# First stage of a decoder step on one core: the first two tiles become forget gates of two heads, with wider loads and one written order per engine

## Chip, cores, metric

The kernel runs on one core of a Trainium2 chip. The metric is the device time of one execution in microseconds (us); the median of the runs shown counts.

## What is computed

One inference step of a single decoder layer for 512 prompt tokens and 8 sample tokens (T = 520 columns), width 1024, all in float32. What matters here is how the layer begins:

```
cs  = silu(c)                                  # 9 conditioning vectors: one of the prompt, eight of the samples
mod = cs @ w_mod + b_mod                       # 6 parts of 1024: sh1, sc1, g1, sh2, sc2, g2
h   = rmsnorm(x) * norm1_g * (1 + sc1) + sh1
u   = h @ w_in                                 # 64 tiles of 128 columns; q, f, i, output gate of 8 heads first
```

From u come an HGRN2 recurrence of eight heads (forget gate f, query q, value i, output gate), an RG-LRU recurrence, two merge gates, the output projection, and after a second norm an MLP with a squared ReLU.

## The kernel before

Activations lie transposed, 128 features by 520 columns, in eight blocks k. Every large product is made of three products of float32r halves (high and low part), two halves of 260 columns each, so one tile of 128 output features takes 8 blocks x 6 matmuls (`products`, L112). A weight tile is loaded (`_load_w`, L72, SP's queue), its high part is a cast on ScalarE (L84) and its low part a subtraction on VectorE (L87); `take_w` (L98) keeps splits two tiles ahead of their use and loads two ahead of the splits.

The first stage is `begin` (L1537). SP's queue loads c, x (four tiles of 128 tokens) and then pieces of w_mod of 256 columns, 1 MB each, scale and shift alternately for blocks 0-1, 2-3, 4-5, 6-7 (`load_mod`, L368); between them stand the weights of the first two tiles, forget gate and query of head 0, 128 columns each. POOL's queue loads small parameters. ScalarE squares x (`norm_x`, L436), VectorE makes the inverse root by a shift and three Newton steps (`rsqrt_small`, L187), TensorE transposes x block by block (`transposed`, L449), and `normed` (L465) scales x into u, which lies in the memory of the untransposed x.

Then follow four rounds, one for each pair of blocks: `mod` (L374) multiplies shift and scale pieces with cs (16 float32 matmuls, recorded as 32), ScalarE copies the result, TensorE transposes it four times and VectorE reduces, adds the bias and multiplies by the gain (`mod_close`, L390). `affine_split` (L479) applies scale and shift: ScalarE writes the high part (L490, with a small one at L494), VectorE a full-precision copy (L495) and the low part (L496). The products of the two first tiles for one pair stand behind the conditioning of the next pair. TensorE's order in this stage is written with `behind`, an order in the program without a wait; the rest is placed by a planner from its own estimate of times. After the last products the pool of the stage is closed, the pool of the heads is opened in its memory, and `head` (L530) starts with two sigmoids on the first accumulator; the PSUM pool `pmm` holds two accumulators.

After that the order is a list of steps, one tile after the other: for each head f, q, output gate, value; after each head two tiles of the RG-LRU. Parts of a head's recurrence are put behind later tiles by `later` (L131): the key transposes (`keys`, L691, transposes at L694) three tiles after the value tile. The value tile's sample rows go through DRAM and come back broadcast to all partitions (`head_sample_v`, L557). The stores of transposed x (L539) are put behind the output-gate tile of head 0.

Of the kernel before, what the change touches and what calls it, by code (L numbers as in the profile page):

```python
# [6 lines left out]
F32 = mybir.dt.float32  # L7
F32R = mybir.dt.float32r
# [7 lines left out]
D = 1024  # L16
L = 512
# [13 lines left out]
NWM = 8  # L31
# [20 lines left out]
class Kernel:  # L52
    def __init__(self, ctx, tc, ins, outs):
# [3 lines left out]
        self.ppt_free = True  # L57
        self.rg_pending = self.turn = self.last_hi = self.split_last = None
# [19 lines left out]
    def _split_w(self, st, place, after=None, after_lo=None):  # L78
# [5 lines left out]
        ins = self.nc.scalar.copy(hi, st)  # L84
        if after:
            self.behind(ins, after)
        ins = self.nc.vector.tensor_tensor(lo, st, hi.bitcast(F32), OP.subtract)  # L87
        if after_lo:
            self.behind(ins, after_lo)
        return hi, lo  # L90

    def split_place(self):

        self.nsplit += 1
        self.places.append(self.nsplit % 4 if self.sw else 2 * (self.nsplit % 3))
        return self.places[-1]

    def take_w(self, key):  # L98
        n = self.wcur
        assert self.wspecs[n] == key, (n, self.wspecs[n], key)  # L100
        while self.wnext_split < min(n + AHEAD + 1, len(self.wspecs)):
# [7 lines left out]
        self.wcur += 1  # L109
        return self.wsplit.pop(n)  # L110
# [127 lines left out]
    def transpose_in(self, out, rows, n):  # L238

        nc = self.nc  # L240
        ps = self.pps.tile([128, 512], F32, name="ps")
        nc.tensor.transpose(ps[:, :n], rows[:n, :], self.ident[:n, :n])
        nc.vector.tensor_copy(out, ps[:, :n])

# [9 lines left out]
    def bounds(self, r):  # L254

        nc = self.nc
        pl = self.hc.tile([128, 16], F32, name="pl")
        self.transpose_in(pl, r, 16)
        hl, lam = pl[:, 0:8], pl[:, 8:16]

        sb = self.hc
        t = sb.tile([128, 10, 8], F32, name="ptmp")
        mx, e, p, lb, na, ex, s, s2, acc, d = (t[:, j] for j in range(10))
        nc.vector.tensor_copy(mx, hl)
        nc.vector.tensor_tensor(e, hl, mx, OP.subtract)
        nc.vector.tensor_scalar(d, lam, -1.0, None, OP.mult)
        nc.vector.tensor_tensor(na, lam, d, OP.min)
        nc.scalar.activation(e, e, AF.Exp)
        self.exps = nc.scalar.activation(ex, na, AF.Exp)
        nc.vector.reciprocal(p, e)  # L270
        nc.vector.tensor_tensor(p, p, e, OP.mult)
        nc.vector.tensor_tensor(lb, p, p, OP.subtract)
        self.lbf, self.lb1, self.c8, self.c8n = (sb.tile([128, 8], F32, name=n) for n in ("lbf", "lb1", "c8", "c8n"))
        nc.vector.tensor_scalar(self.lbf, lb, 1e-30, None, OP.max)
        nc.vector.tensor_scalar(self.lb1, lb, -1.0, 1.0, OP.mult, OP.add)
        self.decay = ex, s, s2, acc, d

    def decays(self):
# [23 lines left out]
    def parameters_mod_in(self, r):  # L302
        pm = self.consts.tile([128, 64], F32, name="pm")
        self.transpose_in(pm, r, 64)
        self.bmod, self.n1g, self.n2g = pm[:, 0:48], pm[:, 48:56], pm[:, 56:64]
        for part in (1, 4):
            c = self.bmod[:, part * 8:part * 8 + 8]
            self.nc.vector.tensor_scalar(c, c, 1.0, None, OP.add)

# [1356 lines left out]
```

## Time and profile before

| | us |
|---|---|
| median of 3 runs | 1012.02 (1011.67 to 1012.32) |
| profiled execution | 1012.27 |
| span of the profile | 1010.5 |
| TensorE busy in the span | 983.7 |
| VectorE, ScalarE busy | 695.6, 516.0 |

The span runs from the first to the last instruction of the profiled execution; 1.8 us of its time lie outside. PE is TensorE (PEld its weight loads), DVE VectorE, ACT ScalarE, POOL GpSimd, SP the engine whose queue issues most loads. TensorE's records are pipelined: a matmul lasts longer than the distance to the next one. The granted clock is given as a share of 2.4 GHz, 0.50 being 1.2 GHz.

### The profile page before, as it was taken

The page shows a single profiled execution, that of the slowest core. Times are in us where ns is not written, and L with a number is a line of the kernel's source. Part 1 is how long each engine was busy: PE and PEld are TensorE (multiplying, and loading weights), DVE is VectorE, ACT ScalarE, POOL GpSimd, SP SyncE. Part 2 cuts the span into 40 slices and gives each one's busy share as a digit, 9 for nine tenths or more (in the row PEclk, how much of TensorE's full clock was granted, in tenths as well). Part 3 has the DMA queues.
Part 4 walks back from the last instruction along what each step waited for, and adds up shares of the span by engine and source line. Part 5 has one row for each costly group of instructions (what it writes and reads, how often), then busy time and mean ns, then how long its engine had stood idle before and what let it go on. Part 6 is the DMA issues. An engine that isn't in the chain of part 4 may idle for free.

```text
span 1010.5 us, 23262 instructions
## 1 busy us (share of the span) xinstructions
PE 983.7 (97%) x9585; PEld 956.7 (95%) x9585; DVE 695.6 (69%) x1545; ACT 516.0 (51%) x985; POOL 108.8 (11%) x193
## 2 busy tenths in 40 slices
PE   5999999999999999999999999999999999999996
PEld 3799999999999999999999999999999999999995
DVE  6778888698878868463233348767767766768775
ACT  5444764574565456351222234466556645646653
POOL 3000000000000000120000000022321331232050
PEclk9899999999999999999999999999999999999998
DMA  9794445354343434586566756222762482283242
GB/s 299 214 261 135 123 129 143 94 154 125 113 131 115 126 91 134 189 271 208 176 188 214 232 167 182 84 84 53 174 150 79 101 197 85 65 183 68 64 84 85
DMA packets 212572, 145.78 MB, mean 144 GB/s; under 512 B 6262, under 2 KB 196878, under 8 KB 212458
## 3 DMA queue, kind: packets, MB, share of 16 engines
q1 hardware_dynamic: 202562, 132.37, 44.3%
q0 software_dynamic: 9904, 11.92, 6.2%
q8 instruction: 75, 1.23, 0.5%
q14 instruction: 31, 0.25, 0.1%
HBM read 123.61 MB, written 13.39 MB: 136 GB/s over the span
## 4 chain that ended last, share of the span: by engine, by line
PE 90%; DVE 3%; DMA 3%; SPq 2%; ACT 1%; issue 1%; DVEq 0%; ACTq 0%
PE mm L118 65%; PE ps L1151 8%; PE pt L1151 4%; PE ps L382 2%; PE pb L1151 2%; PE pb L779 1%; PE ps L628 1%; DMA wm<-in_w_mod_dram 1%; PE mm L1151 1%; PE pt L704 1%; PE pt L717 1%; SPq L75 1%; DMA wst<-in_w_in_dram 1%; DMA xT_d<-ma 1%; SPq L371 1%
## 5 line engine op out<-in xcount | busy, mean ns | idle before, releaser
L118 PE MATMUL mm<-h,whi 128*128 128x260 f32 (+1 forms) x3072 | 508.4, 285 | 1.9 <-ACT X L157 1.2
L118 PEld LDWEIGHTS mm<-h,whi 128*128 128x128 f32 x3072 | 426.3, 189 | 6.8 <-ACT whi L84 1.7
L118 PE MATMUL mm<-h,wlo 128*128 128x260 f32 (+1 forms) x1536 | 314.6, 284 | 0.0
L84 ACT CAST whi<-wst 128x1024 fp32r<-128x1024 f32 x166 | 173.7, 1049 | 211.7 <-PE mm L118 172.5
L87 DVE TENSOR_TENSOR wlo<-wst,whi 128x1024 fp32r<-128x1024 f32 x166 | 202.6, 1221 | 88.3 <-ACT whi L84 87.1
L118 PEld LDWEIGHTS mm<-h,wlo 128*128 128x128 f32 x1536 | 239.8, 189 | 0.1
L118 PE MATMUL mm<-a,whi 128*128 128x260 f32 x512 | 82.8, 283 | 0.0
L118 PEld LDWEIGHTS mm<-a,whi 128*128 128x128 f32 x512 | 70.3, 188 | 0.9 <-issue 0.8
L118 PE MATMUL mm<-a,wlo 128*128 128x260 f32 x256 | 51.7, 284 | 0.0
L1247 DVE TENSOR_TENSOR f<-f 128x260 f32<-128x260 f32 x64 | 27.3, 427 | 28.9 <-ACT f L1242 28.2
L880 POOL DMA_DIRECT2D t<-oaT_d x8 | 4.3, 551 | 375.5 <-DMA oaT_d<-e 368.8
L1236 ACT ACTIVATE ft<-ft,fsh 128x512 f32<-128x512 f32 (+2 forms) x36 | 24.0, 676 | 35.9 <-DVE ft L1233 35.9
L1239 POOL TENSOR_TENSOR ft<-ft,fsh 128x8 f32<-128x8 f32 x28 | 18.5, 660 | 216.1 <-DVE ft L1233 216.1
L118 PE MATMUL mm<-b,whi 128*128 128x260 f32 x256 | 41.6, 284 | 0.0
L118 PEld LDWEIGHTS mm<-a,wlo 128*128 128x128 f32 x256 | 39.4, 188 | 0.0
L118 PEld LDWEIGHTS mm<-b,whi 128*128 128x128 f32 x256 | 35.0, 188 | 2.5 <-issue 2.5
L614 DVE TENSOR_TENSOR Y<-Y,tb 128x512 f32<-128x512 f32 x40 | 27.5, 688 | 11.0 <-ACT Y L616 5.5
L896 DVE TENSOR_TENSOR t<-mm,t 128x520 f32<-128x520 f32 x8 | 5.6, 701 | 37.0 <-PE mm L118 37.0
L1281 POOL DMA_DIRECT2D ma<-snap x28 | 26.1, 932 | 39.8 <-issue 22.3
L1263 POOL DMA_DIRECT2D ma<-snap x28 | 26.1, 932 | 39.0 <-DMA ma<-snap 22.5
L1242 ACT ACTIVATE f<-ft 128x520 f32<-128x520 f32 (+1 forms) x36 | 20.8, 587 | 15.0 <-POOL ft L1240 13.0
L573 ACT ACTIVATE st<-st,fkq 128x128 f32<-128x128 f32 x64 | 19.6, 389 | 14.3 <-DVE fkq L553 12.9
(508 smaller groups left out, 1819.5 us busy)
## 6 DMA issues: line engine op xcount, KB each, us to landing
wst<-in_w_in_dram SPq DMA_DIRECT2D x64, 512.0 KB
wm<-in_w_mod_dram SPq DMA_DIRECT2D x8, 2048.0 KB
wst<-in_w_ff_dram SPq DMA_DIRECT2D x64, 256.0 KB
wst<-in_w_ff_dram SPq DMA_DIRECT2D x32, 512.0 KB
wm<-in_w_mod_dram SPq DMA_DIRECT2D x8, 1024.0 KB
st<-in_state_hgrn_dram SPq DMA_DIRECT2D x8, 512.0 KB
vb<-vd SPq DMA_DIRECT2D x8, 512.0 KB
out_dram<-st SPq DMA_DIRECT2D x8, 512.0 KB
```

The lines of the kernel that those rows point to most:

```text
L84: ins = self.nc.scalar.copy(hi, st)
L87: ins = self.nc.vector.tensor_tensor(lo, st, hi.bitcast(F32), OP.subtract)
L118: self.last_product = self.nc.tensor.matmul(ps[:, s, :c.stop - c.start], x, y[:, c], start=first and n == 0, stop=last and n == 2)
L382: ins = nc.tensor.matmul(ps[r:r + 32, j * n:j * n + n], self.cT[:, k, :], w[:, k, :], start=k < 4, stop=k >= KO - 4)
L573: nc.scalar.activation(st[:, b], st[:, b], AF.Copy, scale=fkq[:, 0, b:b + 1])
L614: made = nc.vector.tensor_tensor(view(Y, b, 0, 2 * b, n, b), view(X, b, 0, 2 * b, n, b), fac, OP.mult)
L1151: ins = self.nc.tensor.matmul(ps, x[:, w], y[:, f], start=j in (1, 7, 2) and k == 0 and n == 0, stop=k == 3 and n == 2, skip_group_check=True)
L1236: nc.scalar.activation(t[:, :p], t[:, :p], AF.Relu, bias=sh[:, 0:1])
L1242: nc.scalar.activation(f, self.two(self.ft)[:, a:a + n], AF.Square)
L1247: self.nc.vector.tensor_tensor(f[:, n], f[:, a], f[:, b], op)
L1263: nc.gpsimd.dma_start(x[1][:, b], v[:, :n], accum_op=OP.add)
L1281: nc.gpsimd.dma_start(x[t][:, a], s[p], accum_op=OP.add)
```

## The change

The first two tiles are the forget gates of heads 0 and 1, whose weights are one load of 256 columns; the query of head 0 becomes the third tile, the first that is taken from the list. The conditioning weights come in pieces of 512 columns: scale of blocks 0 to 3, shift of blocks 0 to 3, (the gate weights,) scale of blocks 4 to 7, and shift of 4-5 and of 6-7 in two halves. Each piece is a session of its own (`session`, `closed`). x is transposed as its tiles arrive, six blocks at once and two later; the root comes from ScalarE's table with one Newton step. The small parameters are transposed into one PSUM tile and copied together. All instructions of the stage on TensorE, ScalarE and VectorE stand in one written order per engine (`order`), in which the products are spread over the sessions. The first weight tile of the list (query of head 0) is split before the last pair of blocks (`split_ahead`). The pool `whe`, the third place of split weights, is opened after the stage, in its memory. The key transposes of head 0 are put two tiles after the value tile. The stores of x stay behind the output gate of head 0, now the second tile after the stage.

The core of the diff:

```diff
-        self.places.append(self.nsplit % 4 if self.sw else 2 * (self.nsplit % 3))
+        self.places.append(self.nsplit % 4 if self.sw else 2 * ((self.nsplit - 1) % 3))
...
-        while self.wnext_split < min(n + AHEAD + 1, len(self.wspecs)):
+        self.split_ahead(min(n + AHEAD + 1, len(self.wspecs)))
+        self.wcur += 1
+        return self.wsplit.pop(n)
+
+    def split_ahead(self, count):
+
+        while self.wnext_split < count:
...
+        order("p", nc.tensor.transpose(ps[:, :16], rl, self.ident[:16, :16]))
+        order("p", nc.tensor.transpose(ps[:, 16:80], rm, self.ident[:64, :64]))
+        order("v", nc.vector.tensor_copy(pl, ps[:, :16]))
+        order("v", nc.vector.tensor_copy(pm, ps[:, 16:80]))
...
+        for r, n in ((ra, 57), (rb, 64), (rc[:, 0], 96), (rc[:, 1], 96)):
+            order("p", nc.tensor.transpose(ps[:, c:c + n], r, self.ident[:n, :n]))
+            c += n
+        order("v", nc.vector.tensor_copy(pa, ps[:, :313]))
...
+        mm = [self.pmm.tile([128, 2, 512], F32, name="mm") for _ in range(2)]
+        rows = [mm[0][:, 0], mm[0][:, 1], mm[1][:, 0], mm[1][:, 1],
+                self.ppb.tile([128, 512], F32, name="pb"), self.ppt.tile([128, 512], F32, name="pt")]
+        for t in range(NC):
+            for k, p in enumerate(rows):
+                order("p", nc.tensor.transpose(p[:, t * 128:(t + 1) * 128], self.xn[:, t, k * 128:(k + 1) * 128], self.ident))
+            if t == 2:
+                between()
...
+        order("a", nc.scalar.activation(r, ss, AF.Sqrt, bias=self.epsc, scale=1.0 / D))
+        h = self.sm.tile([128, 16], F32, name="rs16_h", bufs=2)[:, :8]
+        order("v", nc.vector.tensor_scalar(h, ss, -0.5 / D, -0.5 * EPS, OP.mult, OP.add))
+        self.copied("v", 4, rows[4], order)
+        order("v", nc.vector.reciprocal(r, r))
+        t = self.sm.tile([128, 16], F32, name="rs16_t", bufs=2)[:, :8]
+        order("v", nc.vector.tensor_tensor(t, r, r, OP.mult))
+        order("v", nc.vector.tensor_tensor(t, t, h, OP.mult))
+        order("v", nc.vector.scalar_tensor_tensor(r, t, 1.5, r, OP.add, OP.mult))
...
+        hi = lambda j: order("a", nc.scalar.activation(self.h_hi[:, k0 + j, :L], u[:, k0 + j, :L], AF.Identity,
+                                                       bias=sh[:, j, 0:1], scale=sc[:, j, 0:1]))
+        full = lambda j: order("v", nc.vector.tensor_scalar(f[:, j, :L], u[:, k0 + j, :L], sc[:, j, 0:1], sh[:, j, 0:1], OP.mult, OP.add))
+        lo = lambda j: order("v", nc.vector.tensor_tensor(self.h_lo[:, k0 + j, :T], f[:, j], self.h_hi[:, k0 + j, :T].bitcast(F32), OP.subtract))
+        order("v", nc.vector.tensor_tensor(f[:, :, L:], u[:, ks, L:T], sc[:, :, 1:9], OP.mult))
+        order("v", nc.vector.tensor_tensor(f[:, :, L:], f[:, :, L:], sh[:, :, 1:9], OP.add))
+        hi(0)
+        full(0)
+        order("a", nc.scalar.copy(self.h_hi[:, ks, L:T], f[:, :, L:]))
+        hi(1)
+        between(0)
+        full(1)
+        lo(0)
+        lo(1)
+        between(1)
...
-    def head(self, h, first=None):
+    def head(self, h):
         nc = self.nc
         kf, kq, kv, kg = ([x] for x in self.head_cols(h))
         st = self.head_load(h)
-        f, X = self.head_f(h, first[0] if first else self.gemm(kf, self.h)[:, :, :HALF])
-        q = self.head_q(X[:, 2], first[1] if first else self.gemm(kq, self.h)[:, :, :HALF])
+        f, X = self.first_f[h] if h < 2 else self.head_f(h, self.gemm(kf, self.h)[:, :, :HALF])
+        q = self.head_q(X[:, 2], self.gemm(kq, self.h)[:, :, :HALF])
         ps = self.gemm(kg, self.h)[:, :, :HALF]
-        if first:
+        if h == 0:
...
-        self.later(3, keys)
+        self.later(3 if h else 2, keys)
...
-            steps.append(([kf, kq, kg, kv][2 if h == 0 else 0:], self.head_start if h == 0 else self.head, h))
+            steps.append(([kf, kq, kg, kv][1 if h < 2 else 0:], self.head, h))
...
+        def order(engine, ins):
+            if engine in ends:
+                self.behind(ins, ends[engine])
+            ends[engine] = ins
+            return ins
...
+        def session(part, k0):
+            w = loaded.pop((part, k0))
+            n = w.shape[2]
+            ps = self.pps.tile([128, 512], F32, name="ps")[:, :n]
+            for k in range(KO):
+                r = 32 * (k % 4)
+                order("p", nc.tensor.matmul(ps[r:r + 32], self.cT[:, k, :], w[:, k, :], start=k < 4, stop=k >= KO - 4))
+            ev = self.sm.tile([128, 512], F32, name="modev", bufs=1)[:, :n]
+            order("a", nc.scalar.copy(ev, ps))
+            return ev, part, k0, n // 128
...
+        load(1, 0, 4)
+        load(0, 0, 4)
+        raw = self.start.tile([128, KO, 256], F32, name="wf")
+        nc.sync.dma_start(raw, self.i["w_in"][0][:, D:D + 256].rearrange("(k p) n -> p k n", p=128))
+        load(1, 4, 4)
+        load(0, 4, 2)
+        load(0, 6, 2)
...
+        order("a", self.cond())
+        order("a", nc.scalar.activation(self.act0, self.act0, AF.Sqrt))
+        ss = self.norm_x(order)
...
+        scaled(0, 1, 2, 3)
+        a = session(1, 0)
+        closed(*a)
+        scaled(4, 5, 6, 7)
+        exps()
+        order("a", nc.scalar.activation(self.act0, self.act0, AF.Sigmoid))
+        bounds_end()
+        a = session(0, 0)
+        closed(*a)
+        self.parameters_in(*par, order)
+        high(0)
...
+        self.affine_split(0, order, weights)
+        products((0, 0), (0, 1))
+        a = session(1, 4)
+        self.affine_split(2, order)
+        products((1, 0), (1, 1))
+        closed(*a)
+        a = session(0, 4)
+        products((0, 2))
+        closed(*a)
+        products((0, 3), (1, 2), (1, 3))
+        self.affine_split(4, order)
+        a = session(0, 6)
+        self.last_hi, self.split_last = ends["a"], ends["v"]
+        self.split_ahead(1)
+        ends.update(self.split_ins)
+        products((0, 4), (1, 4))
+        closed(*a)
+        self.affine_split(6, order)
+        products((0, 5), (1, 5), (0, 6), (0, 7), (1, 6), (1, 7))
...
+        self.whe = self.early.enter_context(self.tc.tile_pool(name="whe", bufs=1))
         self.hg = self.open_pool("hg", 2)
-        self.ppt_free = False
+        self.first_f = [self.head_f(h, acc[h][:, :, :HALF]) for h in range(2)]
```

## Rows read from the trace of the kernel before

**Rows 1.** Busy time by stage: window, us, engines (instructions), granted clock, DMA, GB/s.
```profile
27.50:51.00 23.50, 22.69 (x208) 17.66 (x208) 16.72 (x53) 10.67 (x18) 0.04 (x1) 0.90 0.66 197
51.00:120.00 69.00, 67.67 (x827) 66.74 (x828) 52.90 (x157) 35.66 (x80) 0.71 (x3) 1.00 0.61 176
```

**Rows 2.** Timeline of TensorE: start, us, line, tiles, count, idle time before and releaser.
```profile
25.58 1.11 PE L397 MATMUL pt<-ident,modev 128*128 128x128 f32 x4 [3.81 <-ACT modev L385]
...
35.08 1.93 PE L382 MATMUL ps<-wm,cT 128*32 128x256 f32 x32
...
49.24 0.64 PE L118 MATMUL mm<-h,whi 128*128 128x260 f32 x4
...
49.96 0.65 PE L118 MATMUL mm<-h,whi 128*128 128x260 f32 x4
...
52.08 0.75 PE L118 MATMUL mm<-h,whi 128*128 128x260 f32 x4 [1.24 <-ACT X L157]
```

**Rows 3.** Chain of waits up to 130 us: start, us, what.
```profile
17.23 10.16 DMA wm<-in_w_mod_dram
...
27.53 3.64 PE ps L382 x32
...
47.94 2.92 PE mm L118 x22
```

**Rows 4.** Busy time in short windows, around the second conditioning.
```profile
24.00:26.00 2.00, 0.42 (x2) 0.42 (x3) 2.00 (x4) 1.53 (x2) 0.00 (x0) 0.84 1.09 348
26.00:28.00 2.00, 1.17 (x12) 0.60 (x14) 2.00 (x6) 0.00 (x0) 0.00 (x0) 0.50 1.09 348
...
32.00:34.00 2.00, 2.00 (x18) 2.00 (x18) 0.86 (x6) 0.11 (x1) 0.00 (x0) 0.95 1.09 346
```

**Rows 5.** The same, a load of 512 columns and then one of 128.
```profile
535.00:536.00 1.00, 1.00 (x11) 1.00 (x10) 0.00 (x0) 0.00 (x0) 0.00 (x0) 1.00 1.06 403
...
539.00:540.00 1.00, 1.00 (x10) 1.00 (x10) 0.47 (x1) 0.00 (x0) 0.00 (x0) 1.00 1.20 295
```

**Rows 6.** Timeline of ScalarE: last square of x, copy after the third conditioning.
```profile
10.67 1.06 ACT L443 ACTIVATE ht<-xn 128x1024 f32<-128x1024 f32 x1 [0.34 <-DMA xn<-in_x_prompt_dram]
...
37.14 0.59 ACT L385 COPY modev<-ps 128x512 f32<-128x512 f32 x1 [1.12 <-PE ps L382]
```

**Rows 7.** Groups by form, 19 to 51 us: busy us, mean ns, idle before.
```profile
L490 ACT ACTIVATE h<-xn,modT 128x512 fp32r<-128x512 f32 x8 | 6.5, 814 | 8.9 <-DVE modT L409 8.9
...
L496 DVE TENSOR_TENSOR h<-ht,h 128x520 fp32r<-128x520 f32 x8 | 5.5, 699 | 0.9 <-ACT h L494 0.8
...
L477 DVE TENSOR_TENSOR xn<-ma,c 128x520 f32<-128x520 f32 x8 | 5.0, 689 | 0.0
...
L495 DVE TENSOR_SCALAR ht<-xn,modT 128x512 f32<-128x512 f32 x8 | 4.0, 543 | 0.0
...
L1557 DVE TENSOR_TENSOR wlo<-wst,whi 128x1024 fp32r<-128x1024 f32 x2 | 2.4, 1218 | 0.0
...
L385 ACT COPY modev<-ps 128x512 f32<-128x512 f32 x4 | 2.3, 585 | 2.9 <-PE ps L382 2.9
L1556 ACT CAST whi<-wst 128x1024 fp32r<-128x1024 f32 x2 | 2.1, 1036 | 1.1 <-DMA wst<-in_w_in_dram 1.1
...
L402 DVE TENSOR_REDUCE modT<-pt 128x18 f32<-128x72 f32 x8 | 1.5, 227 | 3.7 <-PE pt L397 3.7
L1577 ACT ACT_TABLE_LOAD x1 | 1.3, 1283 | 0.0
...
L405 DVE TENSOR_TENSOR modT<-modT,pm 128x36 f32<-128x36 f32 x4 | 0.8, 196 | 0.1
```

**Rows 8.** Head 0: copy of the value tile, broadcast (chain of waits), key transposes.
```profile
63.91 0.59 ACT L549 COPY e<-mm 128x520 f32<-128x520 f32 x1 [2.54 <-PE mm L118]
...
71.36 5.96 DMA vb<-vd
...
85.18 0.49 PE L694 MATMUL pt<-ident,X 128*128 128x128 f32 x3
```

More of the change, by code (lines that the diff above doesn't have):

```diff
@@ L30 @@
 SESSION = 500
-NWM = 8
 WST = 2
@@ L481, in affine_split @@
+        self.copied("a", 5, rows[5], order)
+        mm = self.pmm.tile([128, 2, 512], F32, name="mm")
+        for j in range(2):
+            for t in range(NC):
+                order("p", nc.tensor.transpose(mm[:, j, t * 128:(t + 1) * 128], self.xn[:, t, (6 + j) * 128:(7 + j) * 128], self.ident))
+        for j in range(2):
+            self.copied("a", 6 + j, mm[:, j], order)
+    def affine_split(self, k0, order, between=lambda j: None):
         nc = self.nc
@@ L1569, in begin, with load @@
-        for k in (4, 6):
-            load_mod(1, k)
-            load_mod(0, k)
-        squares = self.norm_x()
-        self.transposed()
-        self.bounds(pl)
-        self.parameters_mod_in(pm)
-        self.normed()
-        ready = nc.scalar.activation(self.act0, self.act0, AF.Sigmoid)
-        self.behind(self.behind(ready, squares), self.exps)
-        first = [first_w(st) for st in staged]
-        par = self.parameters()
+        loaded = {}
+        def load(part, k, n):
+            loaded[part, k] = w = self.start.tile([128, KO, n * 128], F32, name=f"wm{part}{k}")
+            c = part * D + k * 128
+            nc.sync.dma_start(w, self.i["w_mod"][0][:, c:c + n * 128].rearrange("(k p) n -> p k n", p=128))
@@ new lines, in begin @@
+        load(1, 0, 4)
[5 more added lines that the diff above has]
+        load(0, 6, 2)
+        first = [[self.start.tile([128, KO, 128], F32R, name=f"w{n}{j}") for n in ("hi", "lo")] for j in range(2)]
+        part = lambda j: raw[:, :, j * 128:j * 128 + 128]
+        high = lambda j: order("a", nc.scalar.copy(first[j][0], part(j)))
@@ new lines, in begin, with parameters @@
+        low = lambda j: order("v", nc.vector.tensor_tensor(first[j][1], part(j), first[j][0].bitcast(F32), OP.subtract))
+        order("a", self.cond())
+        order("a", nc.scalar.activation(self.act0, self.act0, AF.Sqrt))
+        ss = self.norm_x(order)
+        bounds = []
+        def parameters():
+            bounds.append(self.parameters_first(pl, pm, order))
+        rows = self.transposed(parameters, order)
+        exps, bounds_end = self.bounds(bounds[0], order)
+        self.normed(ss, rows, order)
@@ L1597, in begin, with weights @@
-        products(sorted(todo))
-        self.parameters_in(*par)
+                self.products(acc[j], (wh[:, k], wl[:, k]), self.h[k], k == 0, k == KO - 1, after=ends["p"])
+                ends["p"] = self.last_product
+        def weights(j):
+            if j == 0:
+                low(0)
+            else:
+                high(1)
+                low(1)
+        self.affine_split(0, order, weights)
+        products((0, 0), (0, 1))
+        a = session(1, 4)
+        self.affine_split(2, order)
```

204 lines of the change are left out of this document (80 added, 124 removed).

## The prediction

> **What bounds the kernel now.** I first read the busy times by stage. From 51 to 120 us TensorE is busy 67.67 of 69.0 us, while before that the stage of the change costs 51 us for two accumulated tiles [rows 1]. So time can only be won or lost where the first two tiles are finished and handed on; what follows is TensorE work that the change leaves alike, six matmuls per block of 128 rows, 0.72 us from one block to the next (49.24 to 49.96) [rows 2]. Then the chain of waits: it runs on a load of the conditioning weights until 27.39, on the second conditioning from 27.53 (3.64 us), and from there on TensorE alone until the last first product at 50.86 [rows 3]. The next matmul starts at 52.08, released by the second sigmoid of ScalarE [rows 2]. So two things bound the stage: arrivals until 27.4, and TensorE's order after it. The clock is a third: TensorE waited 3.81 us before 25.58, the granted clock fell in that stretch and came back around 32 (0.84, 0.50, 0.95) [rows 2, 4], and the second conditioning took 3.64 instead of the 1.93 us of the third [rows 2, 3].
>
> **Loads.** The bytes up to the end of the first weights are the same: 2.2 MB of x and c, 4.2 MB of conditioning, 1.05 MB of gate weights; before, these were all there at 27.39 [rows 3]. Their rows get longer. Rows of 1 KB moved at 348 GB/s [rows 4], a block of 512 columns (2 KB rows) at 403, weights of 128 columns (512 B rows) at 295 [rows 5]. 4.2 MB at 403 instead of 348 is 10.4 instead of 12.05 us; 1.05 MB at 348 instead of 295 is 3.0 instead of 3.55. So the wide gate weights land about 2.1 earlier, at 25.3 (27.39 less 2.1), the shift half 3.0 before that, at 22.3, the scale half 5.2 earlier still, at 17.1. Then scale of blocks 4 to 7 at 30.5, the halves of its shift at 33.5 and 36.5, and the first weight of the next tile at 38.2. The Trainium skill (DMA: Bandwidth & Descriptors, Specifications) gives some 358 GB/s as one core's share of HBM; by that the 2 KB rows would win some 0.35 us in place of 1.65. The 403 of [rows 5] speaks against the page, and the measurement decides.
>
> **What is hidden ahead of 22.3.** The squares of x end at 11.8 before, the last begun at 10.67 [rows 6]; the Sqrt table goes ahead of them, one load of 1.28 [rows 7] in a ScalarE that then waits less, so I take 12.0. The root by table with four small operations replaces twelve small ones. From 12.0 to the closing of the shift at 25.4 VectorE has three copies of 0.7, some sixteen small operations of 0.2, eight scalings (5.0 [rows 7]) and 0.7 of closing: 11 us in 13.4. Two more table loads (Exp, Sigmoid) fall between the two conditionings. I cost all this at nothing: the load of the shift covers it, with 2.4 us to spare; if shift landed earlier than 20, VectorE's 11 us would set the start instead. The parameter transposes (four tiles, one copy) move ahead of the products; they are costed below. Their eight loads are earlier in program order on POOL's queue only. The stores of x on SP's queue move behind one more product tile; weights are requested two ahead of them.
>
> **From 22.3 on**, with 0.05 for each hand-over and the pieces from [rows 2, 7]. Conditioning 1.93, copy 0.59, four transposes 0.5 (1.11 at the half clock), four of the parameters 0.5: 25.9. Reduction and bias are done by then; VectorE's copy of the parameters (313 columns, not in the trace: between the 0.2 of a small operation and the 0.7 of 520 columns; 0.45) ends at 26.4. ScalarE's cast of the gate weights ends then too (25.3 + 1.04). VectorE, in its written order: two small 0.35, full 0.5, low weights 1.22, full 0.5, two lows 0.7 each: 30.4. The products (0,0), (0,1) end at 30.9.
>
> Conditioning of scale 4 to 7: 30.9 to 32.9 (landed 30.5). Its copy stands ahead of the next high parts on ScalarE, 33.5; high 0.81, small 0.2, high 0.81: 35.3; low 36.05. Closing of scale: reduction of four blocks (two cost 0.23; I take 0.3), bias 0.2, gain 0.2: 36.75; closing of shift 0.45: 37.2. High, small, high of blocks 4 and 5 to 39.3, the lows to 40.0. TensorE meanwhile, from 32.9: two products, four transposes, a half conditioning 0.97, one product, two transposes, three products, 38.9, then the last half conditioning, 39.9.
>
> Its copy (256 columns, 0.36) 40.3. **Here the change adds a wait**: the cast of the next tile's weight (1.04, to 41.3) stands ahead of the last high parts on ScalarE, and its low part (1.22, to 42.6) ahead of the last closing on VectorE. Closing 0.45: 43.0. Highs 0.81, 0.2, 0.81; VectorE 0.35, 0.5, 0.5, lows 0.7 and 0.7: 45.1 and 45.8. TensorE has run out of products at 43.0 and waits for these two: (0,6) ends 45.6, (0,7) 46.3, (1,6) and (1,7) 47.8. A matmul outlasts its spacing by 0.16 (0.65 for four that start 0.12 apart), and the copy after the third conditioning began 0.13 after its end at 37.01 [rows 2, 6], not 0.05, which comes three times: **48.2**.
>
> **Sum.** 48.2 instead of 50.86: -2.66. The pause after it (1.22: the pool of the first stage is closed first, so both sigmoids wait for the last product) stays; the weight split early was needed then anyway. 1012.27 of the profiled execution becomes 1009.6; it lies 0.25 above the median of the runs, so **1009.4**. What a measurement of this kernel tells from no change is about 0.2%, 2.0 us. Loads an us earlier or later move the end by about as much (the wait at 30.9 has 0.4 of slack), so this case alone spans 1008.2 to 1010.4. Chance 0.52.
>
> **Rivals.**
> Half clock. TensorE has next to nothing from 25.9 to 29.7 (two matmuls near 27.4). Before, after 3.81 us without work, the clock was at 0.50 until about 32 [rows 2, 4]. If it falls here too, the conditioning of scale takes 3.64 for 1.93, and the products beside it twice their time; +1.7 and +0.6 of it reach the end: 50.5, 1011.7. The same if the clock is still low at 22.3. The Trainium skill (TensorE: Matmul & The Clock Gate, HAM oscillation) says that bursts of matmuls parted by waits for loads begin each time at the half clock, and by it this case is the forecast; the trace agrees for the one gap that was empty, while this gap is not empty. Against it, too: the changed kernel has no empty wait over 2.2 us. Chance 0.24.
>
> Long rows bring nothing. If 403 holds only beside a running TensorE stream, everything that waits for loads comes 1.6 later: 49.8, 1011.0. For it: early in the kernel small loads share the engines. Against it: the rows are the same blocks of the same matrix. The 358 GB/s of the Trainium skill's DMA page would lead nearly here. Chance 0.12.
>
> **Slower.** The value tile of head 0 becomes the third tile after the hand-over instead of the second, while its keys stay at the same tile (two later instead of three). Before, its copy at 63.91 and the key transposes at 85.18 are 21.3 apart, with a broadcast of 5.96 in between [rows 8]. One tile less, 8 x 0.72 = 5.8, leaves 15.5. If the whole chain needs its 21.3, TensorE stands 5.8 at the transposes: 1009.4 + 5.8 = 1015.2. From 4.7 of stall on it is slower than before by over 0.2%. Against it: the transposes are put where their data is expected, other tiles can go first, and the broadcast waited behind other requests. Chance 0.07.
>
> No written order in effect, or the release not tied to the whole pool: then the pause of 1.22 goes too and 1008.0 comes out, or nothing at all changes. Chance 0.05.
>
> **Numbers.** Faster by over 0.2% (below 1010.0): four fifths of the forecast's case, a quarter of the load case and half of the last, 0.47. Slower (over 1014.0): 0.07 for the stall. Within 0.2%: the half clock and the rest, 0.46. The range leaves out the stall and the tail of the half-clock case (both conditionings cold): 1007.6 to 1012.9; the likeliest case alone 1008.2 to 1010.4.
>
> **What would show it.** The first conditioning matmuls near 17, the second near 22.3, both released by a load; some 400 GB/s from 10 to 20 us; the first products at 27.4 and 29.7; a wait of TensorE for low parts near 43 to 45; the last first product near 48.2 and the next tile 1.2 later. The forecast is wrong if the granted clock is 0.50 anywhere between 29 and 34, if shift lands after 24, or if TensorE stands over 1 us between 50 and 100.

## The result and the profile after

The changed kernel takes 1014.15 us (median of 11 runs, 1012.55 to 1016.0) beside 1011.85 (1011.35 to 1012.89) for the kernel before on the same chip: a ratio of 1.0022, interval 1.0015 to 1.003. It is slower by 2.3 us; 1009.4 was forecast, with a range of 1007.6 to 1012.9: the time moved the other way and lies outside the range. The profiled execution is the slowest of the eleven (1016.0, span 1014.1).

The busy times on the page of the changed kernel, beside 983.7, 695.6 and 516.0 before:

```profile
PE 985.5 (97%) x9537; PEld 954.6 (94%) x9537; DVE 693.4 (68%) x1529; ACT 519.1 (51%) x991; POOL 108.8 (11%) x193
```

The timeline of TensorE, changed kernel: the root's transposes, the first and second conditioning, the first products, the third conditioning, two waits for the last pair of blocks, and the first matmul of the next tile, as in [rows 2].

```profile
13.31 1.09 PE L480 MATMUL pb<-ident,rs_y 128*128 128x128 f32 x4 [2.14 <-DVE rs_y L473]
...
16.50 3.35 PE L1583 MATMUL ps<-wm,cT 128*32 128x512 f32 x16
...
22.61 3.47 PE L1583 MATMUL ps<-wm,cT 128*32 128x512 f32 x16 [1.39 <-DMA wm<-in_w_mod_dram]
...
28.95 0.59 PE L121 MATMUL mm<-h,whi 128*128 128x260 f32 x2 [0.90 <-ACT h L500]
31.58 0.80 PE L121 MATMUL mm<-h,whi 128*128 128x260 f32 x2 [2.04 <-DVE h L503]
...
34.05 3.12 PE L1583 MATMUL ps<-wm,cT 128*32 128x512 f32 x16
...
48.48 0.50 PE L121 MATMUL mm<-h,whi 128*128 128x260 f32 x2 [0.67 <-ACT h L500]
49.45 0.51 PE L121 MATMUL mm<-h,whi 128*128 128x260 f32 x2 [0.46 <-DVE h L503]
...
53.59 0.75 PE L121 MATMUL mm<-h,whi 128*128 128x260 f32 x4 [1.24 <-ACT X L160]
```

Its windows of 1 us (columns as in [rows 1]; the clock is the third number from the end):

```profile
12.00:13.00 1.00, 0.00 (x0) 0.00 (x0) 0.93 (x6) 0.95 (x2) 0.00 (x0) 0.80 1.08 381
16.00:17.00 1.00, 1.00 (x7) 0.29 (x9) 1.00 (x2) 0.47 (x1) 0.00 (x0) 0.50 1.04 387
21.00:22.00 1.00, 0.23 (x3) 0.00 (x0) 0.67 (x4) 0.99 (x3) 0.00 (x0) 1.00 1.08 355
24.00:25.00 1.00, 1.00 (x10) 0.27 (x4) 0.92 (x4) 0.00 (x0) 0.00 (x0) 0.50 1.05 380
28.00:29.00 1.00, 0.10 (x2) 0.05 (x1) 0.92 (x5) 0.91 (x2) 0.00 (x0) 1.00 1.04 384
30.00:31.00 1.00, 0.00 (x0) 0.00 (x0) 1.00 (x3) 0.76 (x1) 0.00 (x0) 0.50 1.09 349
34.00:35.00 1.00, 1.00 (x9) 0.30 (x12) 0.48 (x2) 0.00 (x0) 0.00 (x0) 0.50 1.08 345
37.00:38.00 1.00, 1.00 (x11) 0.91 (x8) 0.00 (x0) 0.71 (x2) 0.00 (x0) 1.00 1.21 290
```

Its chain of waits up to the hand-over, as in [rows 3]:

```profile
4.11 18.37 DMA wm<-in_w_mod_dram
22.61 3.49 PE ps L1583 x16
...
34.12 3.04 PE ps L1583 x16
...
45.01 0.96 ACT whi L82
46.00 1.23 DVE wlo L85
49.45 2.92 PE mm L121 x22
```

Read together: the loads came as forecast. The shift weights landed at 22.48 (4.11 + 18.37), and the long rows moved at 375 to 391 GB/s in eight of the ten windows from 10 to 20, instead of 348 [rows 4]. But the granted clock, once up again after each fall, fell three times: in the window from 12, before 24 and before 30. The first fall lies within a wait of TensorE of 2.14 us, the second just behind one of 1.39 us, and the third at a single pair of matmuls that stands between waits of 0.90 and 2.04 us. The clock of 0.50 from 30 to 36 is one of the signs that the prediction named for being wrong. The conditionings that should take 1.93 took 3.35, 3.47 and 3.12. The last first product ended at 52.37 (49.45 + 2.92), not at 48.2, and 1.24 later the next tile began: the **hand-over**, 53.59 instead of 52.08.

In the table, "behind" is the span less the hand-over, that is, everything that the change was not about. Hand-over and "behind" are those of one profiled execution each; the times are medians of 5 to 11 runs (one run for the second profile of the kernel before). The rows come from several chips, so compare the ratios, which are to the kernel before on the same chip, rather than the times.

| run | hand-over | behind | time | ratio (interval) |
|---|---|---|---|---|
| before | 52.08 | 958.4 | 1011.85 | |
| before, second profile | 50.96 | 958.4 | 1011.2 (one) | |
| changed | 53.59 | 960.5 | 1014.15 | 1.0022 (1.0015 to 1.003) |
| changed, again | 53.17 | 959.1 | 1014.16 | 1.0026 (1.0017 to 1.0035) |
| all gaps filled | 49.72 | 958.8 | 1010.59 | 0.9989 (0.998 to 0.9997) |
| last gap filled | 50.92 | 958.8 | 1011.88 | 0.9999 (0.999 to 1.0008) |
| early gaps filled | 51.84 | 959.0 | 1013.21 | 1.0017 (1.0008 to 1.0026) |
| before, gap filled | 50.93 | 958.7 | 1011.55 | 1.0001 (0.9991 to 1.001) |
| forget gate and query | 53.88 | 959.1 | 1013.75 | 1.0016 (1.0007 to 1.0025) |
| state scaling later | 53.90 | 957.8 | 1013.79 | 1.0015 (1.0007 to 1.0024) |
| filled, split late | 49.10 | 957.9 | 1008.85 | 0.9974 (0.9964 to 0.9983) |
| filled, new order | 48.03 | 960.8 | 1010.18 | 0.9987 (0.9978 to 0.9996) |
| new order alone | 51.23 | 963.0 | 1014.86 | 1.0034 (1.0022 to 1.0047) |
| filled, new order, state later | 48.10 | 958.0 | 1007.9 | 0.9964 (0.9952 to 0.9977) |

### The profile page after: what moved, and what is told of

Same layout as the page of the kernel before. It is cut to its first block, busy times and chain, and to the rows that moved or that the text cites. A ratio compares the mean times of both kernels' runs of the same rounds, so it can differ in the third digit from the quotient of the medians.

```text
span 1014.1 us, 23153 instructions
## 1 busy us (share of the span) xinstructions
PE 985.5 (97%) x9537; PEld 954.6 (94%) x9537; DVE 693.4 (68%) x1529; ACT 519.1 (51%) x991; POOL 108.8 (11%) x193
## 4 chain that ended last, share of the span: by engine, by line
PE 88%; DVE 4%; ACT 3%; DMA 2%; issue 1%; SPq 0%; DVEq 0%; ACTq 0%; POOLq 0%
PE mm L121 64%; PE ps L1165 8%; PE pt L1165 4%; PE pb L1165 2%; DMA wm<-in_w_mod_dram 2%; PE ps L384 1%; PE pb L793 1%; PE ps L642 1%; PE ps L1583 1%; PE mm L1165 1%; DVE wlo L85 1%; PE pt L718 1%; PE pt L731 1%; PE pt L733 1%; DMA st<-in_state_hgrn_dram 1%
## 5 line engine op out<-in xcount | busy, mean ns | idle before, releaser
L121 PEld LDWEIGHTS mm<-a,wlo 128*128 128x128 f32 x256 | 39.4, 188 | 0.0
L1295 POOL DMA_DIRECT2D ma<-snap x28 | 26.6, 948 | 40.2 <-issue 22.3
L1277 POOL DMA_DIRECT2D ma<-snap x28 | 26.1, 932 | 39.4 <-DMA ma<-snap 22.8
```

The source lines that it names most:

```text
L121: self.last_product = self.nc.tensor.matmul(ps[:, s, :c.stop - c.start], x, y[:, c], start=first and n == 0, stop=last and n == 2)
L1277: nc.gpsimd.dma_start(x[1][:, b], v[:, :n], accum_op=OP.add)
L1295: nc.gpsimd.dma_start(x[t][:, a], s[p], accum_op=OP.add)
```

## Experiments on the clock

A filler is a matmul that nothing reads: the identity times the conditioning vectors, 256 columns, into a PSUM tile that is free then. It stands in TensorE's written order where TensorE waited.

**All gaps filled.** Four fillers before the root's transposes, two before and five behind the first conditioning, one behind the second, five before the first products.

```diff
+        def filler(dm, n):
+            for _ in range(n):
+                order("p", nc.tensor.matmul(dm[:, :256], self.ident, self.cT.rearrange("p k b -> p (k b)"), start=True, stop=True))
+        filler(self.pps.tile([128, 512], F32, name="ps"), 4)
...
+        dm = self.ppb.tile([128, 512], F32, name="pb")
+        filler(dm, 2)
         a = session(1, 0)
         closed(*a)
+        filler(dm, 5)
...
         a = session(0, 0)
+        filler(dm, 1)
         closed(*a)
         self.parameters_in(*par, order)
+        filler(dm, 5)
```

> The changed kernel with matmuls of no use (identity by the conditioning vectors, into a free PSUM tile) put where TensorE waits: 4 after the first transposes of x, 2 before the first conditioning, 5 before the second, 1 after it, 5 before the first products. Theory 'clock' (the three stretches at the half clock set the end of the stage): the granted clock stays at 1.00 from about 20 us on, the second and third conditionings take 1.9 instead of 3.5 and 3.1 us, the last first product ends at 48.2 to 49.2 instead of 52.4, and the time falls by about 3 us, to 1011. Rival 'order' (the written order and its waits set the end, whatever the clock): the clock is at 1.00, but the last first product stays beyond 51 and the time at 1013 to 1014.

Windows and timeline of TensorE with all gaps filled (the windows as above, then the second and third conditioning, the last products and the next tile):

```profile
24.00:25.00 1.00, 0.99 (x6) 0.30 (x2) 0.00 (x0) 0.53 (x1) 0.00 (x0) 1.00 1.05 385
28.00:29.00 1.00, 0.77 (x5) 0.51 (x3) 1.00 (x2) 1.00 (x2) 0.00 (x0) 1.00 1.04 384
30.00:31.00 1.00, 1.00 (x9) 1.00 (x10) 1.00 (x2) 0.00 (x0) 0.00 (x0) 1.00 1.09 347
```

```profile
22.43 1.92 PE L1583 MATMUL ps<-wm,cT 128*32 128x512 f32 x16 [0.98 <-DMA wm<-in_w_mod_dram]
...
31.37 1.92 PE L1583 MATMUL ps<-wm,cT 128*32 128x512 f32 x16
...
48.08 0.40 PE L121 MATMUL mm<-h,wlo 128*128 128x260 f32 x2
49.72 0.75 PE L121 MATMUL mm<-h,whi 128*128 128x260 f32 x4 [1.24 <-ACT X L160]
```

The clock stays at 1.00, every conditioning takes 1.92, and the last first product ends at 48.48 (48.08 + 0.40; 48.2 was forecast for a full clock). 1010.59 is 3.6 us less than the changed kernel, on another chip; by the ratios it is 3.3 us. So the half clock took the whole loss and more: work that computes nothing makes the kernel faster.

**Which fall costs what.** One run has only the five fillers ahead of the first products, the other only the eleven (4, 2 and 5) before and behind the first conditioning; the single filler behind the second conditioning is in neither.

> The changed kernel with five filler matmuls only in the empty stretch ahead of the first products (no others, so the two earlier falls of the clock stay). Clock theory, with each fall priced alone: the first conditioning's 3.3 us is hidden (the second one waits for the shift weight that lands at 22.4 anyway), the second one keeps its 3.4 to 3.5 us at half clock (1.5 us on the path), the third goes from 3.1 to 1.9 us and the products beside it are at full clock. So last first product at about 50.0 and next tile at 51.2 (52.37 and 53.59 in the changed kernel, 48.48 and 49.72 with all gaps filled); time about 1011.9, no different from before within 0.1%. Rival (the clock's early state decides and later fillers only delay): third conditioning still 3 us, next tile at 53 or later, time 1013.5 or more.

> The changed kernel with fillers only before and behind its first two conditionings (11 of the 17), none ahead of the first products: the complement of the run that filled only that last gap. Clock theory with each fall priced alone: first and second conditioning at 1.9 us, the granted clock falls once, between 28 and 37, third conditioning 2.8 to 3.4 us; hand-over at 49.72 + (53.59 - 50.92) = 52.4, give or take 0.6; time 1012.6 to 1013.6. Rival (the fillers of the early gaps hold the clock through the stage, the last gap does not bring it down): third conditioning at 1.9 us, hand-over before 50.5, time under 1011.2. Other rival (the early gaps cost nothing): hand-over at 53.2 or later, time 1014.

TensorE's timeline with the last gap filled (second and third conditioning, next tile), then with the early ones filled (the same and the second pair of the first products):

```profile
22.31 2.47 PE L1583 MATMUL ps<-wm,cT 128*32 128x512 f32 x16 [2.46 <-DMA wm<-in_w_mod_dram]
...
32.55 1.92 PE L1583 MATMUL ps<-wm,cT 128*32 128x512 f32 x16
...
50.92 0.75 PE L121 MATMUL mm<-h,whi 128*128 128x260 f32 x4 [1.24 <-ACT X L160]
```

Two windows of the same run, during the fillers and behind them:

```profile
28.00:29.00 1.00, 1.00 (x4) 0.82 (x3) 0.97 (x5) 0.67 (x3) 0.00 (x0) 0.50 1.03 377
...
31.00:32.00 1.00, 1.00 (x10) 0.97 (x10) 1.00 (x3) 0.00 (x0) 0.00 (x0) 1.00 1.08 348
```

And with the early gaps filled:

```profile
22.59 1.92 PE L1583 MATMUL ps<-wm,cT 128*32 128x512 f32 x16
...
30.03 0.80 PE L121 MATMUL mm<-h,whi 128*128 128x260 f32 x2 [1.86 <-DVE h L503]
...
32.49 2.89 PE L1583 MATMUL ps<-wm,cT 128*32 128x512 f32 x16
...
51.84 0.75 PE L121 MATMUL mm<-h,whi 128*128 128x260 f32 x4 [1.24 <-ACT X L160]
```

Both came as expected: 1011.88 (1011.9 expected) and 1013.21 (1012.6 to 1013.6). Against the 53.17 of the changed kernel's second profile (below), filling the last gap saves 2.25 us at the hand-over and filling the early ones 1.33; together that is 3.58, and filling all saves 3.45. By the median times the two are 2.3 and 0.95 us, and all together 3.6. So there are two terms on the path, and each can be bought alone; their sizes come from single executions of kernels whose times spread by about 3 us, so they are good to some tenths of a microsecond at best. The fillers of the last gap did not hold the clock up: it had fallen near 23.5, stood at 0.50 through most of the five fillers (0.81 in the window from 30), and was back at 1.00 ahead of the third conditioning. Two sizes differ from what was expected: with the last gap filled the second conditioning took 2.47 us, partly at the full clock, and not 3.4. With the early gaps filled, the clock fell at the single pair of matmuls ahead of the 1.86 us wait (0.84 in the window from 27, 0.50 from 28), and the third conditioning took 2.89.

**The changed kernel once more.**

> The changed kernel itself, once more, on the chip of the next three. Clock theory: the granted clock falls to 0.50 again in the stage before 37 us, by the same empty stretches; the next tile's first product starts 1 to 2.5 us later than in the kernel before (52.08), that is at 53.0 to 54.5; time 1013 to 1014.5, 0.1 to 0.25% above before. Rival (waits of the heads make the loss): the hand-over is at 52 or earlier in this execution, with waits of TensorE of over 1.5 us between 55 and 400 us. If the wait of 0.67 us behind the state scalings and those at 100 to 200 and 349 us of the first profile are absent here while the time stays, they were that execution's own.

1014.16, hand-over 53.17, as expected; this execution ran at the median. It waited longer at first and yet lost less: its first wait (2.79 us, before 13.47) left the clock at 1.00 in the windows from 13 and 16, where the other execution's 2.14 us had been followed by 0.50.

```profile
13.47 0.62 PE L480 MATMUL pb<-ident,rs_y 128*128 128x128 f32 x4 [2.79 <-DVE rs_y L473]
```

```profile
13.00:14.00 1.00, 0.53 (x4) 0.41 (x4) 0.97 (x4) 0.11 (x1) 0.00 (x0) 1.00 1.15 344
16.00:17.00 1.00, 0.86 (x8) 0.29 (x12) 1.00 (x3) 0.38 (x1) 0.00 (x0) 1.00 1.06 391
```

The second and third conditioning were at half clock again (3.57 and 2.91 us). The waits behind the hand-over in the first profile (0.67 and 0.78 us the longest up to 400 us) are absent here (one of 0.5 us for the stores of x stands in their place) while the median is the same, so they belonged to that execution.

**The kernel before, with its gap filled, and once more as it is.** Eight fillers stand in the 3.81 us [rows 2] behind its first conditioning.

```diff
             mod(k)
+            if k == 0:
+                dm = self.ppb.tile([128, 512], F32, name="pb")
+                for _ in range(8):
+                    self.turn = self.behind(nc.tensor.matmul(dm[:, :256], self.ident, self.cT.rearrange("p k b -> p (k b)"), start=True, stop=True), self.turn)
             products(todo[:1])
```

> The kernel before with eight such matmuls of no use between its first conditioning and the transposes behind it, where TensorE waited 3.81 us. Theory 'clock': the granted clock does not fall near 25, the second conditioning takes 1.9 instead of 3.6 us, the last first product ends near 49.0 instead of 50.9 and the time falls by 1.5 to 2.0 us, to about 1010. Rival 'order': what is won there is waited for in the next rounds (VectorE, arrivals), and the time falls by less than 0.5.

> The kernel before, unchanged, for a second profiled execution, since the sum of the loss needs its usual hand-over, and the execution shown of it lies above its median. If its stage varies with where the granted clock falls: the next tile's first product is at 51.0 to 51.8 (52.08 in the execution shown), with 958.4 to 958.8 us behind it in the span as there. If the stage is the same and the variation is elsewhere: the first product within 0.2 us of 52.08 and the span differs behind it.

TensorE's timeline of the kernel before: filled (second and fourth conditioning, next tile), then its second profile (the same):

```profile
27.43 1.93 PE L382 MATMUL ps<-wm,cT 128*32 128x256 f32 x32 [1.17 <-DMA wm<-in_w_mod_dram]
39.39 1.93 PE L382 MATMUL ps<-wm,cT 128*32 128x256 f32 x32 [0.51 <-DMA wm<-in_w_mod_dram]
50.93 0.75 PE L118 MATMUL mm<-h,whi 128*128 128x260 f32 x4 [1.24 <-ACT X L157]
```

```profile
27.09 3.16 PE L382 MATMUL ps<-wm,cT 128*32 128x256 f32 x32 [0.44 <-DVE modT L402]
...
39.42 1.93 PE L382 MATMUL ps<-wm,cT 128*32 128x256 f32 x32 [0.15 <-DMA wm<-in_w_mod_dram]
...
50.96 0.74 PE L118 MATMUL mm<-h,whi 128*128 128x260 f32 x4 [1.24 <-ACT X L157]
```

Here the theory failed and the rival held, since a full clock brings nothing (ratio 1.0001): the fourth conditioning waits for its weights, which land at 39.4, whether the second one took 1.93 or 3.16. In the execution of [rows 2], hand-over 52.08, the clock came back near 32 instead of 29.6; its third conditioning began at 35.08 (33.35 filled, 33.74 in the second profile) and its fourth at 40.54, without a wait. That was too late for the cover. So in the other two executions the kernel before is bound by a landing at 39.4 and has room for a half-clock stretch. In the changed kernel no conditioning after the second waits for a load, so nothing covers one.

## Experiments on the tiles, the heads and the order

**Forget gate and query instead of two forget gates**, with two loads of 128 columns and the keys three tiles later, as before.

```diff
...
-        self.later(3 if h else 2, keys)
+        self.later(3, keys)
...
-            steps.append(([kf, kq, kg, kv][1 if h < 2 else 0:], self.head, h))
+            steps.append(([kf, kq, kg, kv][0 if h else 2:], self.head, h))
...
-        nc.sync.dma_start(raw, self.i["w_in"][0][:, D:D + 256].rearrange("(k p) n -> p k n", p=128))
+        for j, c in enumerate((D, 0)):
+            nc.sync.dma_start(raw[:, :, j * 128:j * 128 + 128], self.i["w_in"][0][:, c:c + 128].rearrange("(k p) n -> p k n", p=128))
...
```

> The changed stage, but its two tiles are forget gate and query of head 0 again (two loads of 128 columns in place of one of 256), with the list of tiles and the keys' place as before. Theory 'states' (with both forget gates ready, the scaling of two heads' states stands on ScalarE ahead of a weight's cast and of the query's sigmoid, and TensorE waits later for what that delays): the end of the stage stays at 52 give or take 1, the waits of TensorE after it, 2.4 us in the changed kernel without the 1.24 at the hand-over, fall under 0.9, and the time is about 1012.5. Rival 'placement' (the later waits come with any new plan): they stay over 2 us and the time at 1014.

1013.75, hand-over 53.88, the half clock again (0.50 in the windows from 28, 31, 34 and 36), 959.1 behind. The waits between 55 and 400 us fell to 0.4, as the theory had it, but in the second profile of the changed kernel they are 0.8 without any edit, and the time came as the rival said. The choice of tiles and the wide load, the change's headline, are not what lost the time: its ratio (1.0016) lies close to those of the changed kernel (1.0022 and 1.0026), and the intervals overlap, so a part of some tenths of a microsecond stays possible.

**State scaling later.** On ScalarE, the sixteen scalings of the states of heads 0 and 1 are put behind the copies of their value tiles.

```diff
-            nc.scalar.copy(self.two(v), ps)
+            self.v_copied = nc.scalar.copy(self.two(v), ps)
...
-            nc.scalar.activation(st[:, b], st[:, b], AF.Copy, scale=fkq[:, 0, b:b + 1])
+            ins = nc.scalar.activation(st[:, b], st[:, b], AF.Copy, scale=fkq[:, 0, b:b + 1])
+            if h < 2:
+                self.behind(ins, self.v_copied)
```

> The changed kernel, but the scaling of the states of heads 0 and 1 is put behind the copy of their value tiles on ScalarE. Theory 'states': the cast that began at 62.90 begins about 5 us earlier, the wait of 0.67 before the third tile after the stage is gone, and 0.7 to 1.8 us of the time: 1012.4 to 1013.5. Rival 'placement': that wait is replaced by others, the time stays at 1014 within 0.5.

1013.79, above the expected 1012.4 to 1013.5 and where the rival put it. The wait of 0.67 is gone and the cast begins at 59.72 instead of 62.90; 957.8 behind the hand-over is 1.3 less than in the changed kernel's second profile, but the time does not show a gain. The same edit is tried again below.

**Split of the next tile late**, all gaps filled: the three lines around `split_ahead(1)` stand behind `affine_split(6, order)`.

> All gaps filled as in the first experiment, and the split of the next tile's weight (cast and subtraction) moved from ahead of the last closing to behind the last affine. Theory (the wait I added is on the path): the cast of 0.9 us and the subtraction of 1.1 us at 41 to 43 us no longer delay the last closing's reduction and affine; the waits of 0.66 and 0.46 us for the last blocks of h at 44.6 to 46 go, last first product at 47.4 to 47.8 (48.48), next tile at 48.8 to 49.5, time 1009.6 to 1010.2. Rival (the split is then late): the next tile's first product waits for its low part, the pause grows from 1.24 to over 2 us, next tile at 49.7 or later, time 1010.6 or more.

1008.85, below the expected 1009.6 to 1010.2. The hand-over moved from 49.72 to 49.10, as expected, and the pause stayed 1.24. Of the two waits for the last blocks of h that of 0.66 is gone, that of 0.46 stayed; 0.9 us more was won behind it, of which 0.4 is the wait for block-diagonal weights at the third tile, gone here. So the wait that the prediction had named cost 0.6 us at the hand-over, and the early split was not needed.

**New order**, all gaps filled: affine of blocks 2 and 3 ahead of the third conditioning, products in ones and twos between conditionings and closings, the split last.

```diff
         self.affine_split(0, order, weights)
         products((0, 0), (0, 1))
+        self.affine_split(2, order)
         a = session(1, 4)
-        self.affine_split(2, order)
-        products((1, 0), (1, 1))
+        products((1, 0))
         closed(*a)
         a = session(0, 4)
-        products((0, 2))
+        products((1, 1))
         closed(*a)
-        products((0, 3), (1, 2), (1, 3))
         self.affine_split(4, order)
+        products((0, 2), (0, 3))
         a = session(0, 6)
-        self.last_hi, self.split_last = ends["a"], ends["v"]
-        self.split_ahead(1)
-        ends.update(self.split_ins)
-        products((0, 4), (1, 4))
+        products((1, 2))
         closed(*a)
         self.affine_split(6, order)
-        products((0, 5), (1, 5), (0, 6), (0, 7), (1, 6), (1, 7))
+        self.last_hi, self.split_last = ends["a"], ends["v"]
+        self.split_ahead(1)
+        ends.update(self.split_ins)
+        products((1, 3), (0, 4), (0, 5), (1, 4), (1, 5), (0, 6), (0, 7), (1, 6), (1, 7))
```

> All gaps filled, and the written order after the first affine changed: the affine of blocks 2 and 3 (its conditioning is long done) is written ahead of the copy of the third conditioning, the products are spread one or two at a time between conditionings and closings, and the split of the next tile's weight stands behind the last affine. Theory (the order, not the amount of work, holds ScalarE and VectorE from 31 to 45 us: h of blocks 2 and 3 sits 4 to 6 us behind a copy it does not need): ScalarE's wait before that copy goes, TensorE has no wait over 0.5 us between 35 and 46, last first product at 46.2 to 47.0, next tile at 47.5 to 48.5, time 1008.4 to 1009.2, 0.25 to 0.35% below before. Rival (the landings and the work bind, 400 GB/s, the last weight at about 36): last first product not before 47.8, time 1009.8 or more. Other rival: the next tile's late split makes the pause over 2 us and gives most of it back.

The hand-over came as expected (48.03), the time did not (1010.18; 1008.4 to 1009.2 expected). Timeline of ScalarE, and TensorE at the third tile:

```profile
53.82 2.45 ACT L587 ACTIVATE st<-st,fkq 128x128 f32<-128x128 f32 x8 [3.87 <-DMA st<-in_state_hgrn_dram]
...
58.92 1.03 ACT L82 CAST whi<-wst 128x1024 fp32r<-128x1024 f32 x1
```

```profile
62.08 0.71 PE L121 MATMUL mm<-h,whi 128*128 128x260 f32 x4 [2.25 <-DVE bdllru_wa L779]
```

ScalarE stood at the state scalings until their load came, behind them stood the cast of a weight, and behind that TensorE, for 2.25 us: what was won at the hand-over was given back 14 us later. **The same order without fillers** and **the same order, filled, with the state scalings later:**

> The changed kernel with the new order of affines and products alone, no filler. If order and clock are separate terms: the clock falls as in the changed kernel (0.50 from 30 to about 36), the order saves the same 1.7 us (49.72 to 48.03 with filled gaps) or less, hand-over at 51.4 to 52.6, and the wait of about 2 us at the third tile's block-diagonal weights is there too, so time 1013.5 to 1015. Rival (the order closes the gaps itself and so holds the clock): no half clock after 31, third conditioning 1.9 us, hand-over before 50.5, time 1012.5 or less.

> The kernel with all gaps filled and the new order of the affines and products, and the state scaling of heads 0 and 1 on ScalarE put behind the copy of their value tiles. Theory: what that order saved at the hand-over (48.03 us there) was given back at the third tile, whose cast (58.92) stood on ScalarE behind sixteen state scalings that had waited 3.87 us for their load, so that TensorE waited 2.2 us for its block-diagonal weights behind it. With the scalings out of the way: hand-over at 48.0 again, that wait gone or under 0.4 us, time 1007.6 to 1008.4 (1010.18 less 2.2). Rival (the loads after the stage come too late by themselves, the tiles of the third product being issued late): the wait stays at 1.5 us or more under the name of another releaser, time 1009.5 or more.

Without fillers the hand-over was 51.23 (third conditioning 2.73, partly at half clock), the wait of 2.3 us was there, and the time was 1014.86: the order does not hold the clock. With both, the timeline of ScalarE and of TensorE reads:

```profile
53.06 0.30 ACT L780 CAST bdhlru_wa<-bdst 128x128 fp32r<-128x128 f32 x1 [3.09 <-DMA bdst<-in_lru_wa_dram]
...
53.93 1.05 ACT L82 CAST whi<-wst 128x1024 fp32r<-128x1024 f32 x1 [0.35 <-DVE bdllru_wx L781]
```

```profile
48.10 0.75 PE L121 MATMUL mm<-h,whi 128*128 128x260 f32 x4 [1.24 <-ACT X L160]
```

The cast starts at 53.93 instead of 58.92, TensorE's wait is gone, and 1007.9 (1007.74 to 1007.95, five runs) beats both kernels: 0.9964 of the kernel before.

## Why the prediction was wrong, point by point

**Right: the loads.** Shift landed at 22.48 (22.3 forecast). The rate was 375 to 391 GB/s, less than the 403 of the forecast and well above 348, so the rival that long rows bring nothing is out.

**Right: the work of the stage at a full clock.** The sum gave 48.2 for the last first product; with all gaps filled it was 48.48. The pause stayed at 1.24.

**Right: the added wait.** The cast and subtraction ahead of the last closing are on the chain (45.01, 46.00), and TensorE waited 0.67 and 0.46 us for the last pair of blocks. Moving the split behind the last affine saved 0.62 us at the hand-over of the filled kernel (49.72 to 49.10); the rest of its gain lies behind the hand-over.

**Wrong: the weight of the half clock, and that it counted once.** This is the step that failed. The forecast's sum takes the second and the third conditioning at 1.93 us each, with the clock up; they took 3.47 and 3.12. The prediction argued against this rival that "this gap is not empty" and that there would be "no empty wait over 2.2 us". The gap between the second conditioning and the first products held one pair of matmuls and the clock fell in it all the same, in both profiles of the changed kernel and in the run with the early gaps filled. One pair of matmuls was no cover in these three. Nor did the second argument hold: the second profile has empty waits of 2.79 and 2.83 us, and the clock fell at the end of the second of them. The rival's own price was fair for one fall (2.3 us; the last gap measured 2.25), but it took the second conditioning at half clock as another form of the same case, when the two are different stretches and add: 1.33 more. Its tail, "both conditionings cold", was left out of the range, and that tail is what happened: 48.48 + 1.33 + 2.25 = 52.06, where the two profiles had 52.37 and 51.93 (the two savings are counted from the second of them).

The Trainium skill (TensorE: Matmul & The Clock Gate, HAM oscillation) says that bursts of matmuls parted by waits for loads begin each time at the low clock. The trace agrees with that for the second conditioning (1.39 us of waiting for its weights, then 3.47 instead of 1.92), and the same happened after waits for ScalarE and VectorE. It doesn't agree with "each time": with the last gap filled the second conditioning followed a wait of 2.46 us for its weights and began with the clock at 1.00 (window from 22), and it took 2.47.

**Wrong by a little: the base.** The forecast subtracted from an execution whose hand-over was 52.08; the second profile had 50.96 with the same 958.4 behind. Half of the difference between the two, 0.56, was gain that the kernel before has by itself in other executions. What bounds it was read from that one execution, too: in the second profile and the filled run TensorE's order after 27.4 is not all, since the load that lands at 39.4 still binds; and in the execution that was read TensorE waited 0.62 us for VectorE just ahead of the 47.94 of [rows 3]. Even at full clock the change is worth 1.1 us (1010.59 beside 1011.71 for the kernel before on that chip), not 2.66: 0.56 is the base, 0.28 the last first product (48.48 for 48.2), some 0.4 the time behind the hand-over (958.8 for 958.4), and 0.3 stays unplaced.

**Wrong by a little: "what follows is TensorE work that the change leaves alike".** Behind the hand-over the changed kernel takes 959.1 (960.5 in the slowest execution) instead of 958.4. Three runs point to ScalarE's order there: with the state scalings later it is 957.8 and 958.0, and with the split's cast later and the scalings where they were it is 957.9.

**The loss, added up.** The second profile of the changed kernel ran at its median, and the mean of the two profiles of the kernel before lies near its median. Their hand-overs, 53.17 less 51.52, differ by 1.65, and behind it 0.7 is lost. That is 2.35 for a measured 2.3 to 2.5.

**The other rivals.** The key transposes of head 0 did not stall: TensorE has no wait at them. The premise of that rival did not come about either: its value tile is copied at 72.11 and its keys are transposed at 93.23, 21.1 us apart as before (21.3), not 15.5. The written order was in effect: TensorE's timeline follows it.

**Open.** What decides in which execution the clock falls after a wait, and when it returns, isn't settled here. That the state scalings are the whole difference behind the hand-over isn't shown either; the run with the late split speaks against it.

## What to carry to other kernels

Where a stage has TensorE in bursts between waits, ask first what the granted clock was before and after each one, and price every stretch of its own; a pair of matmuls in a gap is no proof that the clock holds. A filler matmul in the gap is a cheap probe: if the time falls with the granted clock up, the clock was the bound; if it does not, look for the landing or the engine that covers it. And follow a gain past the hand-over on the other engines: here the order on ScalarE gave back 2.2 us at the third tile, until the instruction that waited for a load was moved behind those that did not.

## What was not expected of the hardware

The same program loses its clock in different places from one execution to the next. In the changed kernel it fell three times in one profile and twice in the other, where a wait of 2.79 us left the clock up; the second conditioning of the kernel before took 3.64 us in one profile and 3.16 in the other. The Trainium skill (TensorE: Matmul & The Clock Gate, Part 1) says of the start of a kernel that the count of matmuls at the low clock varies between runs of one kernel. These runs agree, for a stage of 50 us.

The spread of the times would fit, without being shown to come from this: the changed kernel spreads over 3.45 us (1012.55 to 1016.0), the kernel with all gaps filled over 1.6 (1010.31 to 1011.92), and the best one, also filled, over 0.2 in its five runs. But the filled kernel with the new order alone spreads over 2.3 us (1009.85 to 1012.18), and there the clock is up.
